# Five LayerNorm turns of a fp32 transformer kernel: other work moved out of them, and a cap on the counter that shares weight splits between VectorE and GpSimd

## The chip, the cores and the metric

The kernel runs on one core of one Trainium2 chip. The metric is the device time of one execution in microseconds (us), the median of the runs shown. Engines are called as the profile calls them: PE (TensorE matmul), PEld (its weight loads), DVE (VectorE), ACT (ScalarE), POOL (GpSimd) and SP (SyncE, which issues most transfers).

## The reference

One sequence of 256 tokens, width 1024, goes through two transformer blocks of three sub-blocks each, for a main stream and, at its side, a context stream. All is fp32. A sub-block of the first kind is

```python
h = modulate(x, mod, j)                 # x * (1 + scale) + shift, from the conditions
y = swiglu(h, w_in, w_out)              # or a mixer: pooling, sparse attention, HGRN
x = layer_norm(alpha * x + sub_gate(mod, j) * y, g, b)
```

`mod` and `sub_gate` come from products of a condition vector with large matrices (vector times matrix). The second pair of layers has depthwise convolutions of three taps, gated linear attention, an mLSTM, a state-space layer, and feed-forward parts with a convolution between the products (`conv_ffn`), of which the last ends the kernel.

## The kernel before, in words

**Products.** Every fp32 product is three products of reduced-precision fp32 operands (`mm3`): each operand is split into a high part and a low part. For a weight tile of 128x1024 `wsplit` (L413) does it: ACT writes `wh<-raw`, then `wl<-raw,wh` subtracts on DVE or on POOL. A counter `self.nsplit` grows by `1 / self.lo_pool` at each split, and where it is 1 or more, POOL gets that split and 1 is taken off. `lo_pool` is set for each stage: 4 or 5 in the first block, 2 and 3 in most of what follows, 1.15 in the last stage, `conv_ffn(1)`.

**Order.** A tile framework orders each engine's instructions from the order of the code and a priority heap; the order is fixed when the kernel is built. Each engine works through its own list in that order, so an instruction that waits holds up those behind it.

**A turn.** Between two sub-blocks of the first block stands a chain that nothing of the next sub-block can start without: the last products of `dense_out` (L474) into `acc` banks; on DVE for each of two token halves `acc<-acc,G`, `r<-r,acc`, the statistics, `mv` (mean and variance; the power -0.5 on POOL, L526); `r<-r,mv` on ACT and DVE; eight transposes per half on PE (`aux<-small,r`); the modulation `aux<-aux,mA,mB` on ACT and DVE; and the split into `hTh` (ACT) and `hTl` (DVE), in `to_T` (L505). Then the first products of the next sub-block, `mm<-hTh,...`, can start. There are five such turns (sub-block 0 to 1, ..., 4 to 5); the last has `hlh` and `hll` for `hTh` and `hTl`.

**What else runs there.** (a) The conditions' products ("gemv"): `fill` (L143) collects credit at each step of the main work, and for every `pace` units of it takes one step of a generator: DVE multiplies and adds rows of a loaded matrix (`acc<-graw,cond,acc`, L187; the first of a group `acc<-graw,cond` on ACT), and PE adds over the partitions (`gv<-ones,acc`). (b) The context's products with its split operand `hch`, `hcl`, and the three-tap convolution of the result on DVE (`g<-mm,colv,g`), put behind each turn by `PARKED` (L35): nothing at turn 1, one part at turns 2 and 5, two at turns 3 and 4. Their PSUM tag is `mm` (two banks), the one that the main products use.

**The last stage.** In `conv_ffn(1)` each unit is 48 products into `mm` and `aux`, 16 taps on DVE (`fo<-mm,colv,fo` and `fo<-aux,colv,fo`), and gating (`aux<-fo,aux`, `cg<-aux,cg`). First ten units run alone (about 2664 to 2738 us), then units alternate with the products of the down projection (`acc<-wh,cg`, `acc<-wl,cg`) until 2896 us.

Of the kernel before, what the change touches and what calls it, by code (L numbers as in the profile page):

```python
# [11 lines left out]
F32 = mybir.dt.float32  # L12
# [3 lines left out]
OP = mybir.AluOpType  # L16
# [4 lines left out]
KT = 8  # L21
# [100 lines left out]
class _K:  # L122
# [14 lines left out]


# [4 lines left out]
    def fill(self, units):  # L143

        self.credit += units
        while self.credit >= self.pace:
            self.credit -= self.pace
            next(self.filler, None)
# [25 lines left out]
    def tt(self, out, a, b, op, eng=None):  # L174
        (eng or self.nc.vector).tensor_tensor(out=out, in0=a, in1=b, op=op)  # L175
# [7 lines left out]
    def sub(self, out, a, b, eng=None):  # L183
        self.tt(out, a, b, OP.subtract, eng)
# [18 lines left out]
    def split(self, h, l, src, eng=None):  # L203
        self.act(h, src)
        self.sub(l, src, h.bitcast(F32), eng)
# [207 lines left out]
    def wsplit(self, r):  # L413
# [6 lines left out]
        self.nsplit += 1 / self.lo_pool  # L420
        eng = None
        if self.nsplit >= 1:
            self.nsplit -= 1
            eng = self.nc.gpsimd
# [17 lines left out]
    def dense_T(self, hT, w, c0, n, evac, prep=None):  # L442

        for b in range(0, n, 256):
            m = min(256, n - b)
            r = self.load(self.kcols(w, c0 + b, m) if prep is None else None, (KT, m), prep)
            for i in range(0, m, 128):
                W = self.wsplit(r[:, :, i:min(i + 128, m)])
                p = self.ps([128, hT.h.shape[2]])
                self.prod_T(p[:min(128, m - i)], W, hT)  # L450
                evac((b + i) // 128, p)
                self.fill(1)
                yield
# [20 lines left out]
    def dense_out(self, stat, nk, w, evac, nt=2, both=False, tag="acc"):  # L474
# [8 lines left out]
        for kb, h in steps:  # L483
            m = next((b for b in kbs if b > kb), nk) - kb
            if kb == 0:
# [13 lines left out]
            self.fill(m / 2)  # L499
# [5 lines left out]
    def to_T(self, n, A, B, hT, full=None):  # L505

        for k0 in range(0, KT, 2):
# [12 lines left out]
            self.split(hT.h[:, k0:k0 + 2], hT.l[:, k0:k0 + 2], f)  # L520
        return hT
# [10 lines left out]
    def ffn(self, hT, w_in, w_out, post, tail, more):  # L532

        with self.tc.tile_pool(name="ffn", bufs=1) as fp:
# [17 lines left out]
            self.run(self.dense_out(_Pair(G, L), FT, w_out, post()))  # L552
# [72 lines left out]
    def operand(self, i, hT=None):  # L625

        self.hT = self.pair(self.fbp, KT, T, "hT") if hT is None else hT
        self.to_T(self.cur, *self.mods[divmod(i, 3)], self.hT)
# [120 lines left out]
    def merge(self, l, gp, YH, YL, sgd, post, more):  # L749
# [27 lines left out]
        self.run(self.dense_out(_Pair(MH, ML), KT, I["w_out"][l], post()))  # L777
# [709 lines left out]
    def park(self, i, pool):  # L1487
# [6 lines left out]
        if i < 2:  # L1494
            def ev(k, p):
                k += 2 * o
                out = self.tmp([128, T], "g")
                self.conv3(p, "ml_conv_w_2", i * 4 + k, 8, "ml_conv_b_2", i * 4 + k, out)
                if i:

                    self.ts(out, out, 128 ** -0.5 / 4)
                self.nc.sync.dma_start(dst[:, k], out)
            yield from self.dense_T(self.hc, w, EVEN_OFF["mq"] + i * 512 + o * 256, 256, ev)
# [434 lines left out]
```

## Time and profile before

| what | value |
|---|---|
| runs | 2909.91, 2909.59, 2907.8 us, median 2909.59 |
| the profiled execution | 2907.45 us, span 2905.7 us |
| granted TensorE clock, mean over the span | 0.961 of full speed |
| busy shares of the span | PE 92%, DVE 76%, ACT 44%, POOL 24% |

The span runs from the first to the last recorded instruction; 1.75 us of the profiled execution lie around it. A granted clock of 1.00 is 2.4 GHz and 0.50 is 1.2 GHz; a value between them is the mean of a stretch in which both stood.

### The profile page before, as it was taken

To read this page: it belongs to the slowest core of one execution; us is meant where nothing else is said; L and a number is where in the kernel's file an instruction comes from. 1 tells how busy PE (TensorE), PEld (TensorE's weight loads), DVE (VectorE), ACT (ScalarE), POOL (GpSimd) and SP (SyncE) were. 2 spreads that over 40 slices of the span, in tenths; PEclk is the share of its full clock that TensorE was granted. 3 is DMA by queue.
4 is the path that set the end of the run, shared out by engine and by line. 5 is a ranking of instruction groups with operands and counts; after the bars stand their busy time and mean duration, and the time that the engine had idled before them with its cause. 6 is when DMAs were issued, how large, how long until landed. Compare 5 with 4: busy or idle time off the path is not lost. (4 is left out here: it accounts for less than half of the span.)

```text
span 2905.7 us, 44036 instructions
## 1 busy us (share of the span) xinstructions
PE 2671.4 (92%) x16988; PEld 2375.4 (82%) x16988; DVE 2214.3 (76%) x3955; ACT 1288.7 (44%) x2045; POOL 699.5 (24%) x412
## 2 busy tenths in 40 slices
PE   7998998899999999979999999989999999888888
PEld 7987898799799798978988788778888777666787
DVE  6778798967778898878756767778668468896776
ACT  3445443544444453434446344354333443334444
POOL 1112122112222221221111221212121122233555
PEclk9998999899999998999999999999999999999999
DMA  9898577878788784667856123153223242214343
GB/s 319 300 312 247 190 232 228 261 246 268 253 289 272 254 249 151 210 230 246 283 184 191 48 78 101 59 178 102 88 86 102 73 121 73 80 44 150 126 145 131
DMA packets 402427, 523.24 MB, mean 180 GB/s; under 512 B 24645, under 2 KB 279465, under 8 KB 401321
## 3 DMA queue, kind: packets, MB, share of 16 engines
q1 hardware_dynamic: 400485, 519.69, 55.1%
q8 instruction: 133, 2.18, 0.3%
q10 hardware_dynamic: 1732, 0.74, 0.1%
q14 instruction: 77, 0.63, 0.1%
HBM read 509.32 MB, written 11.07 MB: 179 GB/s over the span
## 5 line engine op out<-in xcount | busy, mean ns | idle before, releaser
L196 ACT ACTIVATE wh<-raw 128x1024 fp32r<-128x1024 f32 x665 | 699.9, 1056 | 945.0 <-PE mm L169 426.4
L175 POOL TENSOR_TENSOR wl<-raw,wh 128x1024 fp32r<-128x1024 f32 x223 | 554.7, 2489 | 1692.5 <-ACT wh L196 1470.2
L175 DVE TENSOR_TENSOR wl<-raw,wh 128x1024 fp32r<-128x1024 f32 (+1 forms) x442 | 551.4, 1249 | 269.3 <-ACT wh L196 265.8
L169 PE MATMUL mm<-hTh,wh 128*128 128x256 f32 (+2 forms) x2200 | 677.8, 309 | 22.1 <-ACT hTh L196 9.0
L169 PE MATMUL mm<-hTh,wl 128*128 128x256 f32 (+2 forms) x2200 | 666.9, 303 | 7.4 <-DVE wl L175 5.9
L169 PE MATMUL mm<-hTl,wh 128*128 128x256 f32 (+2 forms) x2200 | 668.4, 304 | 0.1
L187 DVE SCALAR_TENSOR_TENSOR acc<-graw,cond,acc 128x512 f32<-128x512 f32 x504 | 453.3, 914 | 20.0 <-ACT acc L196 9.0
L169 PEld LDWEIGHTS mm<-hTh,wh 128*128 128x128 f32 (+1 forms) x2200 | 423.3, 193 | 44.1 <-ACT hTh L196 10.4
L169 PEld LDWEIGHTS mm<-hTh,wl 128*128 128x128 f32 (+1 forms) x2200 | 422.5, 192 | 25.3 <-DVE wl L175 7.4
L169 PEld LDWEIGHTS mm<-hTl,wh 128*128 128x128 f32 (+1 forms) x2200 | 423.2, 192 | 17.3 <-issue 2.5
L187 DVE SCALAR_TENSOR_TENSOR fo<-aux,colv,fo 128x189 f32<-128x189 f32 (+3 forms) x396 | 170.4, 431 | 18.1 <-ACT fo L196 14.9
L187 DVE SCALAR_TENSOR_TENSOR fo<-mm,colv,fo 128x189 f32<-128x189 f32 (+3 forms) x396 | 170.1, 430 | 16.9 <-ACT fo L196 14.2
L169 PE MATMUL acc<-wh,gh 128*128 128x512 f32 x352 | 139.9, 398 | 0.9 <-DVE r L175 0.9
L169 PE MATMUL acc<-wl,gh 128*128 128x512 f32 x352 | 139.3, 396 | 0.0
L169 PE MATMUL acc<-wh,gl 128*128 128x512 f32 x352 | 138.8, 395 | 0.0
L169 PE MATMUL mm<-hlh,wh 128*128 128x256 f32 (+1 forms) x456 | 130.9, 288 | 5.7 <-ACT hlh L196 2.9
L169 PE MATMUL acc<-wh,cg 128*128 128x512 f32 x396 | 133.4, 396 | 1.6 <-ACT wh L196 1.6
L169 PE MATMUL aux<-hTh,wh 128*128 128x512 f32 (+1 forms) x352 | 122.9, 349 | 11.3 <-DVE cg L175 11.3
L169 PE MATMUL mm<-hll,wh 128*128 128x256 f32 (+1 forms) x456 | 130.3, 286 | 0.0
L169 PE MATMUL mm<-hlh,wl 128*128 128x256 f32 (+1 forms) x456 | 130.2, 286 | 0.0
L169 PE MATMUL aux<-hTh,wl 128*128 128x512 f32 (+1 forms) x352 | 121.8, 346 | 4.8 <-DVE wl L175 4.8
L169 PE MATMUL aux<-hTl,wh 128*128 128x512 f32 (+1 forms) x352 | 121.0, 344 | 0.0
(554 smaller groups left out, 5488.7 us busy)
## 6 DMA issues: line engine op xcount, KB each, us to landing
raw<-in_ffn_w_in_dram SPq DMA_DIRECT2D x88, 1024.0 KB
graw<-in_w_ada_dram SPq DMA_DIRECT2D x128, 512.0 KB
raw<-in_mix_w_in_dram SPq DMA_DIRECT2D x52, 1024.0 KB
graw<-in_mod_w_dram SPq DMA_DIRECT2D x96, 512.0 KB
raw<-in_ffn_w_up_dram SPq DMA_DIRECT2D x44, 1024.0 KB
raw<-in_ffn_w_out_dram SPq DMA_DIRECT2D x40, 1024.0 KB
raw<-in_even_w_in_dram SPq DMA_DIRECT2D x28, 1024.0 KB
raw<-in_ffn_w_down_dram SPq DMA_DIRECT2D x20, 1024.0 KB
```

The source lines that it names most:

```text
L169: self.nc.tensor.matmul(out, lhsT, rhs, start=start, stop=stop)
L175: (eng or self.nc.vector).tensor_tensor(out=out, in0=a, in1=b, op=op)
L187: self.nc.vector.scalar_tensor_tensor(out, a, s, b, op0=op0, op1=op1, **kw)
L196: self.nc.scalar.activation(out, a, f, **kw)
```

## The change

Four edits, in the order of the diff:

1. `dense_out(..., calm=True)`, which the feed-forward parts and the mixers of the first block and sub-block 5 use: in its last three steps `fill` only collects credit and takes no gemv step. `operand` keeps the last `hTl` instruction of the turn, and the next two gemv steps are issued under `issue_after(turn)`, behind it.
2. `self.calm = 8` at the second-last step: the next eight weight splits go to DVE and none of them to POOL.
3. The context's transposed products take the tag `acc` (three banks) in place of `mm` (two), and their convolutions are issued under `issue_after(turn)`.
4. `self.nsplit` is capped at 1.

```diff
@@ fill
-    def fill(self, units):
+    def fill(self, units, wait=False):
         self.credit += units
-        while self.credit >= self.pace:
+        while self.credit >= self.pace and not wait:
             self.credit -= self.pace
-            next(self.filler, None)
+            with self.after_turn() if self.behind else nullcontext():
+                next(self.filler, None)
+            self.behind = max(0, self.behind - 1)
+    def after_turn(self):
+        return self.tc.issue_after(self.turn)
@@ wsplit
-        self.nsplit += 1 / self.lo_pool
+        self.nsplit = min(self.nsplit + 1 / self.lo_pool, 1)
         eng = None
-        if self.nsplit >= 1:
+        if self.calm:
+            self.calm -= 1
+        elif self.nsplit >= 1:
             self.nsplit -= 1
             eng = self.nc.gpsimd
@@ dense_T
-                p = self.ps([128, hT.h.shape[2]])
+                p = self.ps([128, hT.h.shape[2]], tag)
@@ dense_out
-        for kb, h in steps:
+        for n, (kb, h) in enumerate(steps):
+            if n == len(steps) - 2 and calm:
+                self.calm = 8
-            self.fill(m / 2)
+            self.fill(m / 2, calm and n >= len(steps) - 3)
@@ operand
-        self.to_T(self.cur, *self.mods[divmod(i, 3)], self.hT)
+        self.turn, self.behind = self.to_T(self.cur, *self.mods[divmod(i, 3)], self.hT), 2
@@ the context's products
-                self.conv3(p, "ml_conv_w_2", i * 4 + k, 8, "ml_conv_b_2", i * 4 + k, out)
+                with self.after_turn():
+                    self.conv3(p, "ml_conv_w_2", i * 4 + k, 8, "ml_conv_b_2", i * 4 + k, out)
-            yield from self.dense_T(self.hc, w, EVEN_OFF["mq"] + i * 512 + o * 256, 256, ev)
+            yield from self.dense_T(self.hc, w, EVEN_OFF["mq"] + i * 512 + o * 256, 256, ev, tag="acc")
```

**Turn 1 on DVE.** DVE's list before, from the first half's statistics to the modulation; `acc_2702` is the accumulator of a gemv step, `stats` and `mv` belong to the LayerNorm.

```order
L587 BN_STATS stats<-r 128x6
L187 SCALAR_TENSOR_TENSOR mv<-mv 128x1
L187 SCALAR_TENSOR_TENSOR acc_2702<-graw,cond,acc_2702 128x512
L193 TENSOR_SCALAR r<-r,mv 128x512
L592 BN_AGGR mv<-stats 128x2
L187 SCALAR_TENSOR_TENSOR acc_2702<-graw,cond,acc_2702 128x512
L191 TENSOR_SCALAR mv<-mv 128x1
L187 SCALAR_TENSOR_TENSOR acc_2702<-graw,cond,acc_2702 128x512
L187 SCALAR_TENSOR_TENSOR mv<-mv 128x1
L187 SCALAR_TENSOR_TENSOR acc_2702<-graw,cond,acc_2702 128x512
L193 TENSOR_SCALAR r<-r,mv 128x512
L187 SCALAR_TENSOR_TENSOR acc_2702<-graw,cond,acc_2702 128x512 x2
```

The same stretch of DVE's list in the changed kernel (line numbers of the changed file are 8 to 13 higher; `tof` and `lbe` are another part's set-up):

```order
L605 BN_AGGR mv<-stats 128x2
L199 TENSOR_SCALAR mv<-mv 128x1
L195 SCALAR_TENSOR_TENSOR mv<-mv 128x1
L201 TENSOR_SCALAR r<-r,mv 128x512
L195 SCALAR_TENSOR_TENSOR mv<-mv 128x1
L201 TENSOR_SCALAR r<-r,mv 128x512
L183 TENSOR_TENSOR tof<-lbe 128x512
L183 TENSOR_TENSOR lbe<-lbe,tof 128x1024
L201 TENSOR_SCALAR aux<-aux,mA_87,mB_88 128x256 x2
```

No instruction on `graw` stands between the two halves any more; the first one stands behind the last `hTl`. Two set-up instructions now stand ahead of the modulation.

**Turn 3 on DVE.** Before, the context's convolutions stand between the LayerNorm's instructions:

```order
L191 TENSOR_SCALAR mv<-mv 128x1
L187 SCALAR_TENSOR_TENSOR g<-mm,colv,g 128x255
L187 SCALAR_TENSOR_TENSOR mv<-mv 128x1
L592 BN_AGGR mv<-stats 128x2
L187 SCALAR_TENSOR_TENSOR g<-mm,colv,g 128x255
L193 TENSOR_SCALAR r<-r,mv 128x512
L191 TENSOR_SCALAR mv<-mv 128x1
L175 TENSOR_TENSOR wl<-raw,wh 128x1024
```

In the changed kernel they stand behind the last `hTl` of the turn, alternating with gemv rows, and read `acc`:

```order
L183 TENSOR_TENSOR hTl<-aux,hTh 128x512
L195 SCALAR_TENSOR_TENSOR r<-r,lngb 128x2x512
L183 TENSOR_TENSOR hTl<-aux,hTh 128x512
L195 SCALAR_TENSOR_TENSOR g<-acc,colv,g 128x255
L183 TENSOR_TENSOR mu<-mA_93,colv 128x8
L195 SCALAR_TENSOR_TENSOR acc_7946<-graw,cond,acc_7946 128x512
L195 SCALAR_TENSOR_TENSOR g<-acc,colv,g 128x255
```

The convolutions have left the chain; what they free, the banks of the context's products, is now freed after the turn.

**The last stage.** POOL's list at its end, before (`rsd` belongs to the norms around the stage):

```order
L175 TENSOR_TENSOR wl<-raw,wh 128x1024 x5
L526 TENSOR_TENSOR rsd<-rsd,mhalf 128x2
L175 TENSOR_TENSOR wl<-raw,wh 128x1024 x54
L526 TENSOR_TENSOR rsd<-rsd,mhalf 128x1 x2
L1934 UNCONDITIONAL_BRANCH
```

and in the changed kernel:

```order
L183 TENSOR_TENSOR wl<-raw,wh 128x1024 x4
L539 TENSOR_TENSOR rsd<-rsd,mhalf 128x2
L183 TENSOR_TENSOR wl<-raw,wh 128x1024 x32
L539 TENSOR_TENSOR rsd<-rsd,mhalf 128x1 x2
L1948 UNCONDITIONAL_BRANCH
```

The run of splits on POOL is 32 long where it was 54. The 22 others stand on DVE, among the taps, about six in each group of four units where there were one to two:

```order
L183 TENSOR_TENSOR cg<-aux,cg 128x256
L195 SCALAR_TENSOR_TENSOR fo<-mm,colv,fo 128x3x63
L195 SCALAR_TENSOR_TENSOR fo<-aux,colv,fo 128x4x63
L183 TENSOR_TENSOR wl<-raw,wh 128x1024
L195 SCALAR_TENSOR_TENSOR fo<-aux,colv,fo 128x4x63
L183 TENSOR_TENSOR wl<-raw,wh 128x1024
L195 SCALAR_TENSOR_TENSOR fo<-aux,colv,fo 128x3x63
```

In this piece of DVE's list of the changed kernel two splits stand with one tap between them, and the rest of the unit's taps behind them.

## Rows read from the trace of the kernel before

**Rows 1.** The page: busy times, and granted clock in 40 slices (tenths).
```profile
PE 2671.4 (92%) x16988; PEld 2375.4 (82%) x16988; DVE 2214.3 (76%) x3955; ACT 1288.7 (44%) x2045; POOL 699.5 (24%) x412
PEclk9998999899999998999999999999999999999999
```

**Rows 2.** Stretches: length, busy us of each engine, granted clock, DMA share, GB/s.
```profile
242.00:264.00 22.00, 11.65 (x60) 10.40 (x59) 17.47 (x37) 8.29 (x13) 3.52 (x5) 0.61 0.83 270
553.00:579.00 26.00, 17.88 (x108) 16.17 (x107) 24.28 (x43) 14.15 (x21) 4.78 (x3) 0.74 0.89 281
772.00:800.00 28.00, 21.21 (x156) 19.91 (x154) 26.31 (x49) 16.82 (x27) 4.39 (x3) 0.94 0.73 233
997.00:1019.00 22.00, 18.45 (x148) 17.36 (x147) 19.28 (x40) 14.35 (x23) 4.49 (x5) 1.00 0.76 238
1325.00:1347.00 22.00, 16.76 (x112) 15.00 (x111) 20.21 (x37) 13.10 (x19) 4.44 (x3) 0.84 0.91 280
2664.00:2738.00 74.00, 63.58 (x466) 60.60 (x466) 59.34 (x160) 37.08 (x59) 35.92 (x15) 0.92 0.37 122
2738.00:2896.00 158.00, 140.59 (x862) 125.47 (x862) 101.59 (x257) 68.81 (x103) 95.37 (x39) 0.95 0.42 140
```

**Rows 3.** PE's waits, one turn after another: us in total, times, longest.
```profile
PE aux L512 <- ACT r L196: 9.1, 2, 5.5
...
PE aux L512 <- ACT r L196: 4.9, 1, 4.9
PE mm L169 <- ACT hTh L196: 2.5, 1, 2.5
...
PE mm L169 <- DVE g L187: 6.5, 3, 3.3
...
PE aux L512 <- ACT r L196: 1.9, 1, 1.9
...
PE mm L169 <- ACT hlh L196: 2.9, 1, 2.9
```

**Rows 4.** The stretches of group 2, instructions on `graw` alone: their sum.
```profile
sum 352.00, DVE 26.79 ACT 5.01; mean DVE 3.83 ACT 0.72
```

**Rows 5.** DVE in order of time, in turn 1: start, us, instruction, idle before.
```profile
251.95 0.75 DVE L187 SCALAR_TENSOR_TENSOR acc<-graw,cond,acc 128x512 f32<-128x512 f32 x1 [2.00 <-DMA graw<-in_w_ada_dram]
252.62 0.15 DVE L187 SCALAR_TENSOR_TENSOR mv<-mv 128x1 f32<-128x1 f32 x1
252.73 0.75 DVE L187 SCALAR_TENSOR_TENSOR acc<-graw,cond,acc 128x512 f32<-128x512 f32 x1
253.40 0.54 DVE L193 TENSOR_SCALAR r<-r,mv 128x512 f32<-128x512 f32 x1
253.86 1.53 DVE L187 SCALAR_TENSOR_TENSOR acc<-graw,cond,acc 128x512 f32<-128x512 f32 x2
```

**Rows 6.** DVE, then POOL, in order of time, in turn 2.
```profile
562.78 2.22 DVE L187 SCALAR_TENSOR_TENSOR mv<-mv 128x1 f32<-128x1 f32 x1
...
562.64 2.34 POOL L175 TENSOR_TENSOR wl<-raw,wh 128x1024 fp32r<-128x1024 f32 x1
```

**Rows 7.** DVE's groups of instructions, 2664 to 2896 us: the splits.
```profile
L175 DVE TENSOR_TENSOR wl<-raw,wh 128x1024 fp32r<-128x1024 f32 x9 | 11.0, 1225 | 10.8 <-ACT wh L196 10.8
```

**Rows 8.** PE's waits, first 2664 to 2738 us, then 2738 to 2896.
```profile
PE mm L169 <- DVE fo L187: 4.6, 4, 1.9
PE aux L169 <- DVE cg L175: 3.7, 4, 1.8
...
PE aux L169 <- DVE cg L175: 7.6, 5, 2.4
PE aux L169 <- DVE wl L175: 4.8, 1, 4.8
PE mm L169 <- DVE wl L175: 2.3, 1, 2.3
```

**Rows 9.** DVE and POOL in order of time, in sub-block 1.
```profile
309.71 3.41 DVE L175 TENSOR_TENSOR wl<-raw,wh 128x1024 fp32r<-128x1024 f32 x1
...
309.35 2.70 POOL L175 TENSOR_TENSOR wl<-raw,wh 128x1024 fp32r<-128x1024 f32 x1 [8.20 <-ACT wh L196]
```

More of the change, by code (lines that the diff above doesn't have):

```diff
@@ L1 @@
 import math
-from contextlib import ExitStack
+from contextlib import ExitStack, nullcontext
 from itertools import chain, cycle, islice
@@ L136, in __init__ @@
         self.late = None
+        self.turn, self.calm, self.behind = None, 0, 0
     def dump(self, name, ap):
@@ L174, in tt @@
     def tt(self, out, a, b, op, eng=None):
-        (eng or self.nc.vector).tensor_tensor(out=out, in0=a, in1=b, op=op)
+        return (eng or self.nc.vector).tensor_tensor(out=out, in0=a, in1=b, op=op)
     def mul(self, out, a, b, eng=None):
@@ L183, in sub @@
     def sub(self, out, a, b, eng=None):
-        self.tt(out, a, b, OP.subtract, eng)
+        return self.tt(out, a, b, OP.subtract, eng)
     def stt(self, out, a, s, b, op0, op1, **kw):
@@ L204, in split @@
         self.act(h, src)
-        self.sub(l, src, h.bitcast(F32), eng)
+        return self.sub(l, src, h.bitcast(F32), eng)
     def col(self, name, i, n=1):
@@ L440, in prod_T, with dense_T @@
             self.mm3(p, (W[0][:, k], W[1][:, k]), (hT.h[:, k], hT.l[:, k]), k == ks[0], k == ks[-1])
-    def dense_T(self, hT, w, c0, n, evac, prep=None):
+    def dense_T(self, hT, w, c0, n, evac, prep=None, tag="mm"):
         for b in range(0, n, 256):
@@ L472, in dense_rows, with dense_out @@
             yield
-    def dense_out(self, stat, nk, w, evac, nt=2, both=False, tag="acc"):
+    def dense_out(self, stat, nk, w, evac, nt=2, both=False, tag="acc", calm=False):
         kbs = [0] + list(range(nk % 4 or 4, nk, 4)) if nt == 4 else list(range(0, nk, 4))
@@ L519, in to_T @@
                     self.act(f[:, k], p[:, k], AF.Identity, scale=a, bias=b)
-            self.split(hT.h[:, k0:k0 + 2], hT.l[:, k0:k0 + 2], f)
-        return hT
+            i = self.split(hT.h[:, k0:k0 + 2], hT.l[:, k0:k0 + 2], f)
+        return i.ins
     def rstd(self, out, var, eps):
@@ L551, in ffn @@
                     self.fill(2)
-            self.run(self.dense_out(_Pair(G, L), FT, w_out, post()))
+            self.run(self.dense_out(_Pair(G, L), FT, w_out, post(), calm=True))
             tail(fp)
@@ L776, in merge @@
         self.lo_pool = LO_POOL[l * 3 + 1]
-        self.run(self.dense_out(_Pair(MH, ML), KT, I["w_out"][l], post()))
+        self.run(self.dense_out(_Pair(MH, ML), KT, I["w_out"][l], post(), calm=True))
     def halves(self, x, L):
@@ L1497, in ev @@
                 out = self.tmp([128, T], "g")
-                self.conv3(p, "ml_conv_w_2", i * 4 + k, 8, "ml_conv_b_2", i * 4 + k, out)
-                if i:
-                    self.ts(out, out, 128 ** -0.5 / 4)
+                with self.after_turn():
+                    self.conv3(p, "ml_conv_w_2", i * 4 + k, 8, "ml_conv_b_2", i * 4 + k, out)
+                    if i:
+                        self.ts(out, out, 128 ** -0.5 / 4)
                 self.nc.sync.dma_start(dst[:, k], out)
-            yield from self.dense_T(self.hc, w, EVEN_OFF["mq"] + i * 512 + o * 256, 256, ev)
+            yield from self.dense_T(self.hc, w, EVEN_OFF["mq"] + i * 512 + o * 256, 256, ev, tag="acc")
         else:
```

## The prediction

> **What bounds the kernel now.** I read the page first, then the stretches around the five turns and the last stage, then who makes PE wait in each, and last the order of time where a wait stood out. The reader is to see on the page that PE is busy for 92% of the span and that its granted clock is full in most of the 40 slices [rows 1]: only stretches where PE stands still, or runs at the lower clock, have time to give. The stretches show two such places. In the five turns PE stands still for 22 - 11.65, 26 - 17.88, 28 - 21.21, 22 - 18.45 and 22 - 16.76 us, 34.0 us together, and the clock's mean falls to 0.61 in turn 1 and 0.74 in turn 2 [rows 2]. In the last stage POOL holds most weight splits; PE stands still for 10.4 us of the first 74 and 17.4 us of the next 158 [rows 2].
>
> The waits say what ended PE's idle time. In turns 1, 2 and 4 it is mostly `r`, the normalized rows that the transposes read; in turn 3 it is `g`, the context's convolution that frees a bank; in turn 5 the high half of the operand [rows 3]. All of these come out of DVE's list or stand behind it.
>
> **Turns: what leaves the chain.** Gemv rows took 26.8 us of DVE in these stretches, all of it in the five turns, as the gemv ends before the last stage [rows 4]. What counts is only what stood between the LayerNorm's own instructions.
>
> Turn 1: between the second half's statistics and its `r`, DVE waited 2.00 us for a transfer of `graw` and spent two rows, 0.67 us each from start to start (251.95 to 252.62, 252.73 to 253.40); two more rows, 1.45 us, stood ahead of the modulation [rows 5]. That is 3.3 + 1.45 = 4.8 us. Two set-up instructions now stand ahead of the modulation. An instruction of 128x1024 takes 1.225 us on DVE [rows 7]; as an estimate one half as long takes 0.6, together 1.8 us, of which about 0.8 lies beside the transposes. Net 4.8 - 1.0 = 3.8 us. The first half's wait, most of the longest one of 5.5 us [rows 3], is the chain's own and stays.
>
> Turn 2: a one-column `mv` took 2.22 us because a split on POOL ran from 562.64 to 564.98 [rows 6]; such an instruction takes 0.15 us [rows 5]. The eight splits of edit 2 keep POOL free of splits there: 2.1 us. Convolutions and gemv rows stood between that and the operand, for which PE waited another 2.5 us [rows 3]. Nearly all of these go: I take 2.4. Together 4.5 us.
>
> Turn 3: PE waited 6.5 us for the bank [rows 3]. With three banks and the convolutions behind the turn, the list puts 72 of 96 context products ahead of the operand's first product and 24 behind 43 of them, so this wait must go; but then the LayerNorm chain, which it hid, is what PE waits for. I take half, 3.3 us. Turns 4 and 5 keep a chain of their own; half of 1.9 and of 2.9 us [rows 3] is 1.0 and 1.5 us.
>
> The sum is 3.8 + 4.5 + 3.3 + 1.0 + 1.5 = 14.1 us. Then the clock: PE was busy 11.65 us of turn 1 at a mean of 0.61 [rows 2]; at turn 2's 0.74 the same work takes 11.65 x 0.61 / 0.74 = 9.6 us, so 2 us for a shorter pause. 16.1 us in all.
>
> **Turns: what is given back.** The gemv rows and convolutions are done a few us later, where DVE's splits feed the next sub-block's first products. DVE was busy for 88% to 94% of turns 2 to 5 [rows 2], so it has little room. I take 1 us of PE's waits back, and 8 as the bound: 26.8 us of rows, of which DVE's idle share over the span, 24% [rows 1], hides 6.4, and of the remaining 20 less than half reaches PE. Edit 2 puts some 12 splits more on DVE ahead of the turns, 12 x 1.225 = 15 us; they stand where the gemv steps are held back, so that they replace work of the same size, and cost nothing. If the gemv steps were not held back, they would cost up to the 15. PE's own number of products doesn't change. Turns: -15 us, between -24 (most of the idle time of 34 us, with the clock) and -7.
>
> **The last stage: what edit 4 does there.** With `lo_pool` at 1.15 the counter grows by 0.87 and used to carry its rest over: POOL got 87% of the splits. Capped at 1, it loses the rest each time: 0.87, 1 (taken), 0.87, 1: every second split. With integers (2 to 5 elsewhere) the sum hits 1 exactly and nothing changes. POOL's list confirms it: 54 splits become 32. So 22 splits move to DVE here, 22 x 1.225 = 27 us of DVE time [rows 7].
>
> From below: DVE is idle for 14.7 and 56.4 us in the two stretches [rows 2], more than 27; nothing needs to show. A gain is small, as PE's long waits there are for DVE [rows 8]. From above: all 27 us lie on the chain. In the first stretch about 7 of the 22 are added, 8.6 us, and DVE is 80% busy there; PE waited 8.3 us for its taps and gating [rows 8]. I take 6 us, three quarters, because the units follow each other at DVE's pace and a few splits fall in its waits for ACT. In the second stretch PE is 89% busy, DVE 64%. Fifteen splits are added. PE waited 7.1 us for the seven there, 1.0 each, but two single waits, 4.8 and 2.3, are all of it [rows 8]. At 1.0 it would be 15; I take a third, 5 us, since most of a split's time falls into DVE's idle third. Last stage: +11 us, between 0 and +27.
>
> **Split against split.** A split on DVE that began while POOL had one took 3.41 us, 1.1 us of its own behind the 2.3 us that POOL's still ran [rows 9]. Every second split on DVE means that each follows one on POOL. The Trainium skill (SBUF — State Buffer, section "Who interferes with whom") says that a VectorE instruction with two SBUF inputs contends with a GpSimd instruction that reads SBUF, whoever starts first, and the other fully blocks. The trace agrees, with the 3.41 us. By that rule each of the 22 could cost up to the other's rest as well, rival C below.
>
> **Sum.** -15 + 11 = -4 us, on the profiled execution's 2907.45 us 2903.5. That execution lies 2.1 us under the median of the runs, 2909.59; on the median's scale the result is 2905.6. I say 2905. A difference of 0.2% (5.8 us) is about what a measurement of this kernel can tell from no change.
>
> **Rivals.**
> *A, the forecast* (chance 0.45): both terms about as sized, 2898 to 2912 us.
> *B, the last stage pays nothing* (0.25): DVE's 71 us of idle time take the splits in. For it: a split costs POOL about twice what it costs DVE (35.92 us for 15 [rows 2] against 1.225). Against it: PE's long waits are for DVE's taps, gating and splits [rows 8], all in one list. Then only the turns count: 2909.6 - 15 = 2894.6 us.
> *C, the last stage decides* (0.20), the side opposite to B: DVE works in order, so a split that waits for its `wh` on ACT holds the taps behind it. The nine splits there waited 10.8 us, 1.2 each [rows 7]; and one that starts under POOL's waits for that as in [rows 9]. All 27 us on the chain give 2909.6 - 15 + 27 = 2921.6 us; with a mere 0.5 us of wait for each 2932. It decides from 15 us on, 0.7 us per split.
> *D, the turns give little* (0.10): the LayerNorm chain alone keeps PE waiting, as for the first half in turn 1, or the gemv rows come back as late splits. The turns give 7 us or less, the last stage costs 11: 2909.6 + 4 = 2913.6 us.
>
> **How the numbers follow.** Of A, two fifths lie under 2903.8 (faster by more than 0.2%) and nearly all the rest within 0.2%; B is faster; C is slower; D is half same, half slower. Faster 0.18 + 0.25 = 0.43, same 0.25 + 0.05 = 0.30, slower 0.27. The range goes from 2890, turns at -24 and the last stage at +4, to 2921, where C begins in full; A alone is 2898 to 2912.
>
> **What the profile after would show.** Step by step: no `graw` rows in the five turns and PE's idle time there down from 34 to about 20 us; the one-column `mv` of turn 2 at 0.15 us; no PE wait for `g` in turn 3; a clock above 0.61 in turn 1; about 31 splits on DVE from the up phase on where there were 9, and the stretch from 2664 to the end of the products about 11 us longer than 232. The prediction is wrong if the last stage keeps its length, or grows by over 20 us, or if PE's idle time at the turns stays above 28 us or comes back as waits for `wl` on DVE in the 20 us behind them.

## The result and the profile after

The changed kernel takes 2940.06 us (median of 4 runs, 2937.82 to 2944.79) against 2908.7 us of the kernel before (4 runs, 2900.54 to 2909.91): a ratio of 1.0116, 95% interval 1.0092 to 1.0140. It is about 31 us slower, outside the range that was given. The profiled execution took 2937.82 us, span 2936.0, granted clock 0.954.

The page of the changed kernel, busy times and granted clock:

```profile
PE 2681.3 (91%) x16988; PEld 2385.7 (81%) x16988; DVE 2239.6 (76%) x3988; ACT 1286.7 (44%) x2044; POOL 616.3 (21%) x379
...
PEclk9998999999999979999999999999999999998999
```

TensorE did the same number of products (x16988). It was busy for 10 us longer than before (2681.3 against 2671.4), at a lower mean clock, and idle for 20 us more (254.7 of the span against 234.3). Both parts make up the loss.

The stretches that answer to [rows 2]; columns as there. Turn 2's row runs from the product that stands at 553 us before to the one at 579; the others are moved by about what the kernel had lost up to there. Turn 4 has two rows, and the first begins some 10 us ahead of the turn:

```profile
242.00:264.00 22.00, 10.42 (x48) 8.78 (x47) 17.33 (x28) 10.79 (x15) 1.92 (x4) 0.69 0.29 94
559.80:580.70 20.90, 14.89 (x100) 13.53 (x99) 17.77 (x28) 12.83 (x18) 4.38 (x3) 0.84 0.65 202
775.00:803.00 28.00, 22.29 (x158) 20.73 (x157) 24.44 (x41) 12.84 (x19) 4.72 (x3) 0.88 0.47 148
1006.00:1028.00 22.00, 21.97 (x137) 19.33 (x137) 14.46 (x24) 11.01 (x14) 2.42 (x3) 0.96 0.69 215
1028.00:1050.00 22.00, 9.08 (x51) 8.47 (x50) 17.77 (x29) 5.89 (x11) 3.94 (x3) 0.67 0.70 205
1350.00:1372.00 22.00, 16.32 (x115) 15.23 (x114) 19.23 (x31) 13.10 (x19) 5.25 (x3) 0.84 0.50 159
2691.00:2765.00 74.00, 58.43 (x419) 56.01 (x419) 62.61 (x157) 32.84 (x53) 19.90 (x8) 0.89 0.34 111
2765.00:2926.00 161.00, 146.40 (x911) 129.69 (x909) 120.47 (x282) 73.55 (x108) 57.65 (x24) 0.97 0.43 142
```

The reader is to see that turn 2 is better (20.9 us for the work that took 26, PE idle for 6.0 us where it was 8.1, clock 0.84 for 0.74), that turn 1 is not (PE idle for 11.6 us, 10.35 before), and that behind turn 4 there is a new hole: PE idle for 12.9 of 22 us. The last stage, which was to cost 11 us, is only about 3 us longer (74 + 161 us to the same product for 74 + 158).

To see where the time went, the same product was looked up in each trace by its name and number (the n-th `mm<-hTh,wh`, `acc<-wh,gh` and so on), and the lengths between such products subtracted. In us against the kernel before, from one execution of each kernel; edit 1 alone, edit 1 moved later, edits 3 and 2 alone are experiments below:

```
stretch of before            changed  edit 1  later  edit 3  edit 2
   0.0- 240.4                  +0.3    +2.9   +2.8    -1.6    -1.0
 240.4- 273.7 turn 1           +2.4    +1.8   -4.1    -0.4    -0.4
 273.7- 551.6 sub-block 1      +4.2    +5.9  +34.2    +4.0    -2.5
 551.6- 580.7 turn 2           -5.5    -5.0   -5.4    +2.0    -4.4
 580.7- 772.4 sub-block 2      +2.0    +5.2   +0.8    -2.4    -1.3
 772.4- 836.5 turn 3           +9.1    +5.8   -3.3    +1.1    +3.0
 836.5- 982.6 sub-block 3      -3.1    -6.2   -4.3    -1.7    -1.0
 982.6-1200.5 turn 4, mixer   +11.0    +9.0   +2.3    +4.6    -3.5
1200.5-1312.4 mixer's rest     +4.7    +2.0   -1.5    +2.3    +2.7
1312.4-1372.9 turn 5           +3.5    +8.5   +3.5    +0.1    -2.4
1372.9-1540.7 sub-block 5      -0.9    +2.4   +9.3    -2.3    +0.6
1540.7-2660.5                  -1.0    +1.6   +7.3    +8.2    +4.5
2660.5-end    last stage       +3.3    -2.9   -1.8    +6.8    -7.1
```

Some caution is due: the stretch 1540.7 to 2660.5 is the same code in all of them, and differs by up to 8 us between these executions. An experiment below, in which only the counter is set at the head of the last stage, has the lists of before up to there; its one execution differs from before by -5.1 us in the row "turn 4, mixer" and by +12.3 us from 1540.7 to 2660.5. A single entry of a few us shows nothing by itself. In the changed kernel, though, 27 of the 30 us lie between turn 1 and sub-block 5, turns 3 and 4 ahead.

**Turn 4.** TensorE's waits from 1006 to 1050 us of the changed kernel, then ACT and DVE in order of time (start, us, instruction, idle before):

```profile
PE mm L177 <- ACT g L204: 12.4, 1, 12.4
```

```profile
1036.42 0.39 ACT L204 ACTIVATE acc<-g 128x256 f32<-128x256 f32 x1 [2.31 <-DVE g L195]
1043.12 0.38 ACT L204 ACTIVATE g<-mm 128x256 f32<-128x256 f32 x1 [6.32 <-DMA mlk<-g]
```

```profile
1034.86 0.47 DVE L195 SCALAR_TENSOR_TENSOR g<-acc,colv,g 128x255 f32<-128x255 f32 x1
1035.25 0.74 DVE L195 SCALAR_TENSOR_TENSOR acc<-graw,cond,acc 128x512 f32<-128x512 f32 x1
...
1037.95 0.28 DVE L199 TENSOR_SCALAR g<-g 128x256 f32<-128x256 f32 x1
1038.15 7.37 DVE L195 SCALAR_TENSOR_TENSOR acc<-graw,cond,acc 128x512 f32<-128x512 f32 x11
```

Read backwards: the sub-block's first product waits 12.4 us for a bank of `mm`. The bank holds the context's second part, whose rows ACT copies out (`g<-mm`). The copy waits for a buffer `g`, which is free when the convolution's result in it has been stored (`mlk<-g`). That convolution now stands behind the turn, with gemv rows in between: it ends at 1038.2, its store lets go at 1043.1. Something that was put behind the turn holds, through a buffer, a bank and a copy, what the turn leads up to.

Nine more us are lost ahead of this turn. From 993.5 to 1008.4 us stand products of `dense_out` that took 5.6 us before (984.1 to 989.7). TensorE waits 2.4 us there for a split on GpSimd (the last section has it), does 16 sums of gemv rows, and its granted clock, 1.00 in the same stretch before, falls to 0.79. Columns as in [rows 2]:

```profile
992.00:1002.00 10.00, 7.56 (x31) 6.08 (x29) 5.18 (x6) 1.78 (x2) 4.33 (x1) 0.79 0.65 212
```

At the end of the operand's first products the kernel is 33 us behind; the mixer that follows makes up for some 13 of them, so that the table has +11.0.

**Turn 1.** DVE in order of time, in turn 1 of the changed kernel:

```profile
249.46 0.68 DVE L183 TENSOR_TENSOR tof<-lbe 128x512 f32<-128x512 f32 x1
250.18 1.23 DVE L183 TENSOR_TENSOR lbe<-lbe,tof 128x1024 f32<-128x1024 f32 x1
251.32 1.03 DVE L201 TENSOR_SCALAR aux<-aux,mA,mB 128x256 f32<-128x256 f32 x2
...
254.78 1.28 DVE L183 TENSOR_TENSOR hTl<-aux,hTh 128x512 fp32r<-128x512 f32 x2
255.98 3.34 DVE L723 RECIPROCAL tof<-tof 128x512 f32<-128x512 f32 x1
259.24 0.91 DVE L201 TENSOR_SCALAR aux<-aux,mA,mB 128x256 f32<-128x256 f32 x2
```

The gemv rows are gone, and the mixer's set-up of a bound (`lbe`) has moved up into the turn: a reciprocal of 3.34 us now stands between the operand's first and second part. The place that was cleared in DVE's list did not stay empty; other ready work took it. What the reciprocal costs is not shown: on ACT the second half's `hTh` also stands behind a split that waits for TensorE until 261.33 us.

TensorE's list shows where the +2.4 us of the table come from. Of the changed kernel, then of before:

```profile
254.68 0.58 PE L177 MATMUL mm<-wh,hTh 128*128 128x256 f32 x1 [3.48 <-ACT hTh L204]
273.52 0.28 PE L177 MATMUL mm<-hTh,wh 128*128 128x256 f32 x1
...
275.47 1.05 PE L177 MATMUL gv<-ones,acc 128*128 128x1 f32 x8 [1.45 <-DVE acc L195]
276.39 0.37 PE L177 MATMUL mm<-hTh,wh 128*128 128x256 f32 x1
```

```profile
257.24 0.56 PE L169 MATMUL mm<-wh,hTh 128*128 128x256 f32 x1
273.26 0.39 PE L169 MATMUL mm<-hTh,wh 128*128 128x256 f32 x1
...
273.72 0.28 PE L169 MATMUL mm<-hTh,wh 128*128 128x256 f32 x1
```

The next sub-block's first product comes 2.8 us earlier, measured from the products where the row begins (240.4 us before, 240.7 now). A wait for the operand's second part and the lower clock use that up until 273.5 us. Then eight sums of gemv rows, which stood at the head of the turn before, stand between two products that followed each other, and TensorE waits 1.5 us for them.

### The profile page after: what moved, and what is told of

It is laid out like the page before. It is cut to its first block, busy times and chain, and to the rows that moved or that the text cites. A ratio compares the mean times of both kernels' runs of the same rounds, so it can differ in the third digit from the quotient of the medians.

```text
span 2936.0 us, 44019 instructions
## 1 busy us (share of the span) xinstructions
PE 2681.3 (91%) x16988; PEld 2385.7 (81%) x16988; DVE 2239.6 (76%) x3988; ACT 1286.7 (44%) x2044; POOL 616.3 (21%) x379
## 5 line engine op out<-in xcount | busy, mean ns | idle before, releaser
L183 POOL TENSOR_TENSOR wl<-raw,wh 128x1024 fp32r<-128x1024 f32 x190 | 474.0, 2495 | 1673.1 <-ACT wh L204 1519.8
L183 DVE TENSOR_TENSOR wl<-raw,wh 128x1024 fp32r<-128x1024 f32 (+1 forms) x475 | 592.4, 1249 | 255.8 <-ACT wh L204 254.3
L177 PE MATMUL mm<-wh,hTh 128*128 128x256 f32 x384 | 117.8, 307 | 22.4 <-ACT g L204 12.4
L177 PE MATMUL aux<-hTh,wh 128*128 128x512 f32 (+1 forms) x352 | 120.3, 342 | 11.6 <-DVE cg L183 11.5
```

The lines of the kernel that those rows point to most:

```text
L177: self.nc.tensor.matmul(out, lhsT, rhs, start=start, stop=stop)
L183: return (eng or self.nc.vector).tensor_tensor(out=out, in0=a, in1=b, op=op)
```

## The experiments

All times are medians; a difference is taken against the kernel before in the same set of runs (2906.3 to 2907.7 us). The traces are of one execution each, which lies up to 12 us from its kernel's median.

**Each edit taken out of the changed kernel.** The edits; the first leaves the cap in all other stages, and so does every kernel below that is built with it:

```diff
# without the cap in the last stage
-        self.nsplit = min(self.nsplit + 1 / self.lo_pool, 1)
+        self.nsplit += 1 / self.lo_pool
+        if self.lo_pool > 1.5:
+            self.nsplit = min(self.nsplit, 1)
# without the splits on VectorE
-                self.calm = 8
+                self.calm = 0
# without the hold and the queue
-            self.fill(m / 2, calm and n >= len(steps) - 3)
+            self.fill(m / 2)
-        self.turn, self.behind = ..., 2
+        self.turn, self.behind = ..., 0
# without the context's edit
-ev, tag="acc")
+ev)
-                with self.after_turn():
+                with nullcontext():
```

> The changed kernel, with the cap on the counter taken away in the last stage alone (lo_pool 1.15), so that GpSimd gets 87% of its splits again. Theory M (the loss arises at the turns of the first block; the last stage cost 3.4 us in the two traces): about 3 us shorter than the changed kernel, 2937 us, with the last stage as long as before. Rival, the sum of the prediction (the last stage costs 11): 2929 us. Rival C: 2913 us.

Measured: 2927.5 us, ratio 1.0083 (1.0060 to 1.0105), 20.5 us over before. Against the changed kernel's 31 that is some 11 us less; the two intervals together leave anything from about 0 to 19. The expectation was too small: it took the 3.3 us by which the changed kernel's last stage differs from that of before, but without the cap that stage is 3.7 us shorter than before, not as long, since the eight splits ahead of the turns leave another value in the counter. The two traced last stages differ by 7.1 us. The prediction's own term of 11 fits.

> The changed kernel, without the eight splits in front of each turn that go to VectorE: GpSimd gets its usual share there. Theory M: within 4 us of the changed kernel's 2940, as the long waits after it are not for these splits; the one-column mv of a turn is held up by GpSimd again, 2 us at turn 2. Rival (VectorE is short of time at the turns, and the splits moved to it are what it lacks): 8 to 15 us shorter, 2925 to 2932 us.

Measured: 2961.99 us, 1.0195 (1.0172 to 1.0218), 55 us over before and 22 over the changed kernel. Neither theory had this. The trace shows where it is: 17 us of it in the last stage, which this edit does not touch except through the counter's value. The next experiment takes that up.

> The changed kernel, with the conditions' products where they were: no credit held back, and none of them queued behind the turn. Theory M: the 12.4 us wait at turn 4 stays, since it comes from the context's convolutions behind the turn; the burst of rows behind turns 1, 3 and 5 goes, 8 us shorter, 2932 us. Rival (the held rows are what costs, by the backlog on VectorE and late transfers): 25 us shorter, 2915 us, and the wait at turn 4 is gone.

Measured: 2903.9 us, 0.9998 (0.9982 to 1.0014). The whole loss is gone without edit 1, more than the rival's 25 us. Turn 4 is not cured, as its waits show: the 12.4 us wait became one for the conditions' rows, and one for `hTl`. TensorE's waits of that kernel, 1005 to 1035 us:

```profile
PE gv L177 <- DVE acc L195: 7.9, 1, 7.9
PE aux L525 <- DVE hTl L183: 5.4, 1, 5.4
```

> The changed kernel, with the context's convolutions as before: in the mm banks, and not queued behind the turn. Theory M: the 12.4 us wait at turn 4 is gone, and with the clock and turns 3 and 5 it is 15 us shorter, 2925 us. Rival (held rows): the wait at turn 4 stays and at most 4 us go, 2936 us.

Measured: 2924.24 us, 1.0071 (1.0047 to 1.0095), 17 us over before. The context's edit costs 14 to 16 us of the changed kernel's loss, as theory M had it, and the wait of 12.4 us is gone; but it is the smaller part.

**Which splits fall to VectorE in the last stage.**

```diff
         self.lo_pool = 1.15
+        self.nsplit = 0.2
```

> The changed kernel, with the counter set to 0.2 at the head of the last stage, so that GpSimd and VectorE change places in the alternation: the same number of splits, but the other ones of each unit, in the order that stood in the kernel without the eight splits. Theory P (which of a unit's splits falls to VectorE decides; it explains that kernel's 256 us of last stage against 239): 17 us longer than the changed kernel, about 2957 us, with PE's waits for a split on VectorE at about 20 us in the last stage. Rival (the eight splits ahead of the turns are worth 22 us at the turns themselves): within 4 us of the changed kernel.

Measured: 2956.58 us, 1.0169 (1.0145 to 1.0193), as theory P had it. The number of splits on each engine is the same within one (31 and 32), their turns are swapped. TensorE's waits in the last stage, first of the changed kernel (2691 to 2926 us), then of this one (2688 to 2950):

```profile
PE aux L177 <- DVE cg L183: 11.5, 5, 3.3
PE mm L177 <- ACT cg L204: 7.1, 3, 2.7
...
PE acc L177 <- DVE wl L183: 1.3, 3, 0.9
```

```profile
PE aux L177 <- DVE wl L183: 19.6, 5, 4.6
PE aux L177 <- DVE cg L183: 17.1, 8, 3.4
```

Five splits of a unit's second product stand behind taps on DVE, and TensorE waits 19.6 us for them. So, measured from the kernel without the cap in this stage, the cap costs about 11 us in one phase and some 28 in the other, and the phase is set by whatever ran through the counter before, in the first block too.

**Edit 1 alone, on the kernel before.** The diff is edit 1's part of the one in front.

> The kernel before, with edit 1 alone: credit held in the last three steps of each output product, and the next two steps of the conditions' products queued behind the turn. Theory H (the held rows alone are the loss): 17 to 29 us slower than before, about 2928 us. Rival HC (they cost little alone, and much only with the context's convolutions queued behind the same turn, since both then take VectorE in turns): within 6 us of before, and no PE wait of over 6 us at turn 4.

Measured: 2933.64 us, 1.0094 (1.0071 to 1.0117), 26.9 us slower: theory H. TensorE waited 18.7 us in 9 waits for sums of gemv rows, where before had 3.9 us; the longest is at turn 4. Its waits from 240 to 1590 us, and DVE in order of time at turn 4:

```profile
PE gv L172 <- DVE acc L190: 18.7, 9, 7.7
...
PE gv L172 <- DVE mod L190: 8.9, 5, 5.5
```

```profile
1030.27 0.69 DVE L178 TENSOR_TENSOR hTl<-aux,hTh 128x512 fp32r<-128x512 f32 x1 [1.30 <-ACT hTh L199]
1030.88 11.49 DVE L190 SCALAR_TENSOR_TENSOR acc<-graw,cond,acc 128x512 f32<-128x512 f32 x14
...
1043.74 1.22 DVE L178 TENSOR_TENSOR wl<-raw,wh 128x1024 fp32r<-128x1024 f32 x1
```

A whole step, 14 rows, runs in one piece behind the last `hTl`: 11.5 us in which the sub-block's first split on DVE waits its turn, and TensorE, which has the sum of these rows in its list, waits too. Over the whole execution TensorE is idle for 17 us more than before and busy for 14 us longer with the same products (2685.8 us for 2671.4): about half of the loss is waits, the other half the lower clock. Late loads are a small part at most: DVE waited 10.3 us for `graw` between 240 and 1590 us, and 6.2 before.

**A buffer of its own for the context's rows, in the changed kernel.**

```diff
             def ev(b, m, t, p):
-                out = self.tmp([128, T], "g")
+                out = self.tmp([128, T], "gv")
```

> The changed kernel, with a buffer tag of their own for the context's rows at turn 4, so that ACT's copy out of the bank does not wait for the convolutions' buffers and their store. If that chain (first product of the sub-block, bank, copy, buffer, store, convolution behind the turn) makes the 12.4 us wait at turn 4: the wait is gone and the time is 6 to 11 us shorter than the changed kernel, 2931 us. If the bank is held by something else: the wait stays and the time is within 4 us of it.

Measured: 2934.44 us, 1.0094 (1.0074 to 1.0113): 27.7 over before, 3 to 6 us less than the changed kernel. The chain was the right one, since the wait for the bank is gone, but most of its time only changed hands. TensorE's waits of this kernel from 985 to 1075 us:

```profile
PE gv L177 <- DVE acc L195: 11.8, 2, 7.0
```

**Edits 2 and 3, without 1 and without the cap in the last stage.** The changed kernel with the first and the third edit of the list above.

> Edits 2 and 3 alone: the eight splits on VectorE ahead of each turn, and the context's convolutions in the acc banks and behind the turn; the conditions' products where they were, and the cap not in the last stage. If the held rows and the alternation in the last stage are the two losses: 4 to 12 us under the kernel before, about 2898 us. Rival (the context's edit costs by itself at turn 4): 2907 to 2912 us.

Measured: 2896.42 us, 0.9965 (0.9951 to 0.9980), 10.4 us faster than before, as expected.

**The two halves of edit 1, each alone.**

```diff
# wait only
-        self.turn, self.behind = ..., 2
+        self.turn, self.behind = ..., 0
# behind only
-            self.fill(m / 2, calm and n >= len(steps) - 3)
+            self.fill(m / 2)
```

> The kernel before, with one half of edit 1: credit is held back in the last three steps, but nothing is queued behind the turn. With both halves it was 27 us slower than before. If the rows that bunch up after the hold are the loss: 15 to 27 us slower than before. If the queue behind the turn is: within 8 us of before.

Measured: 2908.1 us, 1.0009 (0.9990 to 1.0029).

> The kernel before, with the other half of edit 1: no credit held back, but the next two steps of the conditions' products after each turn are queued behind its last hTl on VectorE. If the queue is the loss (TensorE's list has the sums of these rows early, and waits for them): 15 to 27 us slower than before. If the hold is: within 8 us of before.

Measured: 2914.87 us, 1.0023 (1.0009 to 1.0038), 7.3 us slower. Neither half makes the 27. The traces show why: from 25 us ahead of the first `hTl` to the last one of each turn (`hll` in the fifth), DVE did 14, 11, 2, 10 and 13 gemv rows before, 13, 8, 3, 12 and 4 with the credit held alone, 7, 1, 0, 8 and 7 with the queue alone, and 1, 1, 1, 1 and 0 with both. Only together do they keep the rows out of the turn, and all of these must then stand behind it.

**TensorE's sums without their wait.** Both kernels have this edit:

```diff
-                self.mm(p[:, i, k:k + 1], acc[:, k * 128:(k + 1) * 128], self.ones1)
+                self.mm(p[:, i, k:k + 1], self.ident, self.ones1)
```

> The control for the next kernel: the kernel before, with TensorE's sums over the partitions reading a constant in place of the rows that VectorE has multiplied, so that TensorE never waits for these rows; the conditions' values are not computed. All rows, loads and sums are still done. TensorE waited 11 us for these rows and their followers between 240 and 1590 us: 3 to 12 us faster than before.

> The kernel before with edit 1 alone (27 us slower than before), and with TensorE's sums reading a constant as in the control; the conditions' values are not computed. If TensorE's wait for its own sums of held rows (34 us between 240 and 1590 us in that kernel, 11 before) and the clock that falls with it are the loss: within 8 us of the control. If VectorE's burst of rows delays the splits and the rest of the turn instead: 15 us or more over the control.

Measured: the control 2935.63 us, 1.0099 (1.0073 to 1.0125), 28 us slower than before; with edit 1 2914.97 us, 1.0023 (1.0008 to 1.0038). The pair is inconclusive. Without the dependence the lists come out in another order, and the control gets slower, with other waits (15.1 us for `gl` where before had 5.5, 8.8 us for splits on DVE); in the second one TensorE's wait went to the next link, the bank of `gv`, which waits for `mod` on DVE:

```profile
PE gv L172 <- DVE mod L190: 18.5, 6, 7.7
```

**The queued steps moved later.** Edit 1 alone and the changed kernel, with credit taken off at each turn (5 and 7 units):

```diff
         self.turn, self.behind = ..., 2
+        self.credit -= 5
```

> The kernel before with edit 1 alone (27 us slower than before), and with 5 units of credit taken off at each turn, so that the queued steps of the conditions' products come later: TensorE's first sum then stands 124, 145, 131, 139 and 240 products behind the five turns in its list, where edit 1 alone has 103, 103, 60, 70 and 111. If TensorE's wait for sums of rows that are queued behind the turn is the loss: at most 10 us slower than before, and no wait of over 4 us for these rows. If the hold itself costs (rows bunched up, late loads): 20 us or more slower than before.

> The changed kernel, with 7 units of credit taken off at each turn: the first sum 142, 172, 169, 56 and 192 products behind the turns, where the changed kernel has 97, 89, 75, 25 and 111. By the theory of the sums: 8 to 20 us shorter than the changed kernel, 2920 to 2932 us, with the wait at turn 4 left (the context's buffers). If the hold itself costs: within 4 us of the changed kernel.

Measured: 2938.14 us, 1.0107 (1.0076 to 1.0137), 31.8 us slower than before; and 2929.54 us, 1.0082 (1.0057 to 1.0106), 23.2 us slower, 8 us less than the changed kernel's loss. The second lies at the edge of what the theory of the sums expected, with the wait for the context's buffer left at turn 4 (10.4 us); the first goes against it. The table in front shows why: with edit 1 later, turn 1 goes from +1.8 to -4.1 us, turn 3 from +5.8 to -3.3 and turn 4 from +9.0 to +2.3, but sub-block 1, the mixer, goes from +5.9 to +34.2 (in the slowest of this kernel's four runs). The waits for the sums have moved: the longest is 3.8 us, but there are 9.6 us of them in that mixer. TensorE's waits of the later kernel, 272 to 585 us:

```profile
PE gv L172 <- DVE acc L190: 9.6, 4, 3.8
```

Gemv rows in the mixer's stretch, in the kernel before (273.7 to 551.6 us), with edit 1 alone, and with it later (DVE, ACT, clock, DMA share, GB/s):

```profile
273.70:551.60 277.90, 77.69 (x93) 9.83 (x14) 0.97 0.69 220
```

```profile
278.40:562.20 283.80, 84.13 (x98) 10.54 (x15) 0.94 0.70 223
```

```profile
272.50:584.60 312.10, 95.21 (x108) 11.36 (x16) 0.90 0.65 213
```

Rows that are not done ahead of a turn are done in the mixer behind it: 6 us more of them and 6 us more time with edit 1, 17.5 us more of them and 34 us more time with the later one. The same three stretches with all instructions, columns as in [rows 2]:

```profile
273.70:551.60 277.90, 252.63 (x1917) 237.04 (x1916) 240.60 (x447) 130.00 (x236) 56.90 (x41) 0.97 0.69 220
```

```profile
278.40:562.20 283.80, 260.94 (x1919) 244.78 (x1920) 237.02 (x447) 127.54 (x234) 56.05 (x40) 0.94 0.70 223
```

```profile
272.50:584.60 312.10, 274.89 (x1936) 255.22 (x1936) 246.49 (x461) 131.84 (x239) 59.46 (x41) 0.90 0.65 213
```

DVE does not run out of time there: it is busy for 240.6, 237.0 and 246.5 us. TensorE is busy for 252.6, 260.9 and 274.9 us with nearly the same number of products, at a granted clock of 0.97, 0.94 and 0.90. With edit 1 the lower clock is all of the 6 us; with the later one it is 22 of the 34, and 12 are idle time. That the rows cause the pauses is argued from the waits for their sums, not shown apart.

**Edits 2 and 3, each alone, on the kernel before.** The kernel of edits 2 and 3, with the context's edit taken out as in the list, or with the splits.

> The kernel before with edit 2 alone: the eight splits ahead of each turn on VectorE. Edits 2 and 3 together were 10 us faster than before. If the splits make it (no split of GpSimd's holds up the one-column mv at turn 2, 2 us, and likewise elsewhere): 5 to 10 us faster than before. If the context's edit does: within 4 us.

Measured: 2889.4 us, 0.9942 (0.9923 to 0.9962), 16.9 us faster, more than expected. TensorE's waits, 553 to 579 us, which hold turn 2:

```profile
PE mm L177 <- ACT hTh L204: 3.4, 1, 3.4
PE aux L527 <- ACT r L204: 1.7, 1, 1.7
```

Before, the same waits were 2.5 and 4.9 us [rows 3]. The one-column `mv` is free of GpSimd's splits, as said, but the eight splits are one too few: a ninth goes to GpSimd within the turn, and DVE's `r` takes 2.57 us beside it, where one takes 0.54 [rows 5]. DVE, then GpSimd:

```profile
558.61 2.57 DVE L201 TENSOR_SCALAR r<-r,mv 128x512 f32<-128x512 f32 x1
```

```profile
557.97 2.92 POOL L183 TENSOR_TENSOR wl<-raw,wh 128x1024 fp32r<-128x1024 f32 x1 [0.62 <-ACT wh L204]
```

> The kernel before with edit 3 alone: the context's products in the acc banks, their convolutions queued behind the turn. If it makes the gain of edits 2 and 3 (no wait for a bank at turn 3, 6.5 us in before): 5 to 10 us faster than before. If the splits do: within 4 us, with the waits gone at turn 3 and come back at turn 4.

Measured: 2920.35 us, 1.0045 (1.0027 to 1.0062), 14.0 us slower. The wait for the bank at turn 3 is gone, and at turn 4 there is another. TensorE's waits, 1010 to 1030 us:

```profile
PE gv L177 <- DVE acc L195: 10.4, 1, 10.4
```

So edit 2 makes the gain of edits 2 and 3, and edit 3 costs some of it: 6.5 us by the medians of these two kernels, which have the same order of splits in the last stage. Alone it costs more, and part of that is not its own. Its last stage is 6.8 us longer than before, with an order of splits that no other kernel here has. The cap that this kernel keeps in the other stages is the one change that bears on the counter: with the cap, a rest of the counter can be lost where `lo_pool` changes.

**The counter alone.** On the kernel before and on edit 2 alone:

```diff
         self.lo_pool = 1.15
+        self.nsplit = 0        # on the kernel before
+        self.nsplit = 0.6      # on edit 2 alone
```

> The kernel before, with the counter set to 0 at the head of the last stage, which gives that stage the order of splits that it has with edit 2 alone. If the order makes the 7 us: 5 to 9 us faster than before, with a last stage of about 235 us. If not: within 3 us.

> Edit 2 alone, with the counter set to 0.6 at the head of the last stage, which gives that stage the order that it has before. If the turns make the rest: 8 to 12 us faster than before, with a last stage of about 242 us. If the counter makes all of the 17 us: within 4 us of before.

Measured: 2900.15 us, 0.9975 (0.9959 to 0.9991), 7.5 us faster than before; and 2891.34 us, 0.9950 (0.9931 to 0.9968), 16.3 us faster. The first says that the value of the counter is worth 7 us. The second says that edit 2 loses at most a few us of its gain when the counter's value is that of before. The two don't add up, and their intervals allow it; that the turns make the larger part of edit 2's gain is what both leave. Edit 2 alone, at 2889.4 us, is the fastest kernel of the study by its median; the interval of the last one overlaps with its own.

The traces of all kernels show the same. The length of the last stage, from the product at 2660.5 us to the last product, goes by the order of splits on DVE. Eight executions with the order of before took 230.3 to 239.6 us (mean 235.0), four with that of edit 2 alone 227.8 to 231.5 (229.0), five with that of the changed kernel 238.6 to 240.8 (239.5), two with the swapped one 255.9 and 259.2. So the cap costs 4.5 us against before, and 10.5 us against the order that the kernel has when the cap is taken out.

## Why the prediction was wrong

The sign was wrong, and the step that failed first is "turns: what is given back", with its 1 us. Edit 1, which keeps the gemv steps out of the turns, costs 26.9 us by itself, what it gains there already taken off. TensorE's idle time at the turns, which was to fall from 34 to about 20 us, is 42 us (five turns by the rows above, turn 4 with both of its rows).

- **What leaves the chain of the turn.** The mechanism of edit 2 was right for the one-column `mv`: it takes 0.16 us or less in the changed kernel, and turn 2 is 5.5 us shorter (4.5 was said). That this is edit 2's doing is not shown: turn 2 is 5.0 us shorter with edit 1 alone, where GpSimd's split began behind the last `mv`, and 4.4 with edit 2 alone. The kernel with edit 2 alone is 17 us faster, near the -15 us for the turns, in part by luck: 7 us of it lie in the last stage, through the counter. For the gemv rows, 26.8 us of them [rows 4], the prediction counted what stood between the LayerNorm's instructions and took it as gained. At turn 1 3.8 us were to be gained. The first product behind the turn does come 2.8 us earlier, and the whole row is 4.1 us shorter where the sums come later; in the changed kernel it is 2.4 us longer, since the operand's second part, the lower clock and the sums take the gain back.
- **What is given back.** The bound was 8 us. It was reckoned from DVE's idle share over the whole span, 24% [rows 1]. The rows do not spread over the span: they run behind the turn, 14 of them in one piece of 11.5 us at turn 4 of edit 1 alone, and then in the mixer. The hold and the queue behind the turn cost 0.5 and 7.3 us apart and 26.9 together. The prediction priced the rows as time of DVE. The loss is not there, as DVE's busy time in the mixer hardly changes: TensorE waits for sums of these rows, which stand in its list ahead of what it could do meanwhile, and its clock is lower in the stretches with such pauses. The waits for the sums and the lower clock are what the prediction did not have.
- **Turn 3 and the context.** "This wait must go" was right (no wait for `g` at turn 3 in the changed kernel), and the gain of 3.3 us was not: in the changed kernel turn 3 is 9.1 us longer, and edit 3 costs 14 us alone and 6.5 beside edit 2. The prediction looked at the banks and not at the buffer that the deferred convolution writes. At turn 4 that buffer, two deep, links the deferred convolution back to the first product.
- **The clock.** A gain of 2 us was said. Turn 1 and 2 are better (0.69 for 0.61, 0.84 for 0.74), and the hole behind turn 4 takes it back (0.67). Over the span the clock falls from 0.961 to 0.954, and TensorE is busy for 10 us longer.
- **The last stage.** +11 us was the forecast, and taking the cap away there gives 11 us by the medians. Against the kernel before the traces show only 3 to 5 us, as without the cap this stage would have been some 6 us shorter than before. That it depends on the counter's phase by 17 us more was not seen: the prediction counted splits and not which split of a unit moves. Nor does the cap change "nothing" in the other stages: it alters what the counter carries into this one. Rival C's price for a split that meets POOL's did not show: the 31 splits on DVE in the changed kernel took 1.207 to 1.230 us. In the swapped phase the longest took 1.66.
- **The sum.** Alone, edit 1 costs 26.9 us and edit 2 gives 16.9; edit 3 costs 6.5 beside edit 2, and the cap 11 where the others stand. That is 27.5, near the 31 measured. That fits, though the experiments that take one edit out show that they are not quite independent: out of the changed kernel edit 3 takes 14 us.

Not settled: how edit 1's 27 us divide between the waits for sums and the rows in the mixers, since each experiment that moved the one moved the other too. Of the 14 us of edit 3 alone about half lies in the last stage's order; where the other half arises is open, since its entries in the table are no larger than the differences between executions of the same lists.

## What to carry to other kernels

Work that is pushed off a critical stretch has to be given a place: ask what its engine does in the stretch behind, who in another engine's list waits for its result, and which buffer it keeps; "later" is the beginning of the next busy stretch, not the idle time of the average. And a cleared place in an engine's list can be refilled by the scheduler with whatever is ready, as here with a 3 us reciprocal. Where a counter carries over from stage to stage, set it at the head of each stage: its phase can be worth more than its share.

## What the runs showed of the hardware

In the changed kernel a split on GpSimd took 7.10 us, near three times its usual 2.4. GpSimd, then DVE, in order of time, ahead of turn 4:

```profile
989.23 7.10 POOL L183 TENSOR_TENSOR wl<-raw,wh 128x1024 fp32r<-128x1024 f32 x1 [8.81 <-ACT wh L204]
```

```profile
987.62 5.37 DVE L195 SCALAR_TENSOR_TENSOR acc<-graw,cond,acc 128x512 f32<-128x512 f32 x8
992.92 1.21 DVE L183 TENSOR_TENSOR wl<-raw,wh 128x1024 fp32r<-128x1024 f32 x1
```

While DVE went through eight rows and a split without a break, GpSimd's split began among them and ended 2.2 us after DVE's split (996.33 to 994.13 us), about its usual length later; TensorE waited 2.4 us for it. [Rows 6] and [rows 9] show the other direction, DVE held by GpSimd. This agrees with the rule that the prediction cites (the Trainium skill, SBUF — State Buffer, section "Who interferes with whom"): it names no engine that always wins, and says that the order of issue decides. That a whole train of DVE instructions keeps GpSimd waiting, and not only the one that runs when its split begins, is how this row reads. One before reads the same way: a split on GpSimd that began at 974.45 us, among five gemv rows and ahead of a split on DVE, took 4.13 us and ended 2.2 us behind DVE's split (978.58 to 976.34 us). A burst on DVE is thus a cost for GpSimd's splits too, which the prediction had not priced.
